# A rotary embedding on one core: 2 MiB units with 16 KB rows, in-place fp16 arithmetic, and fp32 stores from SyncE

## The chip, the cores and the metric

The kernel runs on one core of a Trainium2 chip. The metric is the time of one execution on the device in microseconds (us), taken over several runs. The span is the stretch that a profile covers; it is about 1.8 us shorter than the time of the same run (84.2 against 86.0 for the kernel before). Here VectorE and ScalarE compute, TensorE multiplies small matrices in the setup, and GpSimd, SyncE and ScalarE issue transfers, which the core's 16 DMA engines carry between HBM (the large memory, where input and output lie) and on-chip memory.

## The reference, cut to what matters

```python
# x: (8, 8, 1024, 64) fp32, freqs: (32,) fp32, positions: (1024,) int, scale: 0.5
angles = np.outer(positions * scale, freqs)          # (1024, 32)
cos, sin = np.cos(angles), np.sin(angles)
x_first, x_second = x[..., :32], x[..., 32:]
out_first  = x_first * cos - x_second * sin
out_second = x_first * sin + x_second * cos
return np.concatenate([out_first, out_second], axis=-1)   # fp32
```

Input and output are 16.78 MB each. The tables of cosine and sine are the same for all 64 heads, so they are built once.

## The kernel before

It works in 16 units of 1 MiB (4 heads; a partition holds 8 KB of fp32). Unit 0 comes as fp32 through SyncE; the others are loaded by GpSimd, whose transfers convert to fp16 on the way in and back to fp32 on the way out.

```python
nc.sync.dma_start(out=X0, in_=xv[:, 0, :])
for h in range(HEADS):                                   # 4 small loads
    nc.scalar.dma_start(out=pos_i64[h*HP:(h+1)*HP, :], in_=positions...)
nc.scalar.dma_start(out=freq_row, in_=freqs[None, :])
for g, n in enumerate((1, 1, 2, 2, 3, 3, 3)):            # all loads at the start
    nc.gpsimd.dma_start(out=X, in_=xv[:, u0:u0 + n, :])  # fp32 -> fp16
# ... y = position * frequency, two range reductions, cosT and sinT by ScalarE ...
for u in range(NU):
    nc.vector.tensor_tensor(out=pc, in0=X, in1=cos_b, op=ALU.mult)
    nc.vector.tensor_tensor(out=ps, in0=X, in1=sin_b, op=ALU.mult)
    nc.vector.tensor_tensor(out=OUT[:, :, 0, :], in0=pc[:, :, 0, :], in1=ps[:, :, 1, :], op=ALU.subtract)
    nc.vector.tensor_tensor(out=OUT[:, :, 1, :], in0=ps[:, :, 0, :], in1=pc[:, :, 1, :], op=ALU.add)
    nc.gpsimd.dma_start(out=ov[:, u, :], in_=OUT)        # fp16 -> fp32
```

## Time and profile before

| | before |
|---|---|
| time, median | 85.94 us (85.92 to 86.07) |
| span | 84.2 us |
| VectorE busy | 63.6 us, 72 instructions |
| sine table's first reader on VectorE starts | 14.36 us |
| last store issued | 72.60 us |

The prediction below shows the lines of the profile and reads them. In these lines DVE is VectorE, ACT ScalarE, POOL GpSimd, SP SyncE, PE TensorE and PEld its weight load; a q behind a name is the engine's sequencer. A line of a timeline gives start and duration in us, engine, line of the kernel, operation, what is written <- what is read, and in brackets how long the engine was idle before and what ended that.

### The profile page before, as it was taken

The page shows a single profiled execution, that of the slowest core. Times are in us where ns is not written, and L with a number is a line of the kernel's source. Part 1 is how long each engine was busy: PE and PEld are TensorE (multiplying, and loading weights), DVE is VectorE, ACT ScalarE, POOL GpSimd, SP SyncE. Part 2 cuts the span into 40 slices and gives each one's busy share as a digit, 9 for nine tenths or more (in the row PEclk, how much of TensorE's full clock was granted, in tenths as well). Part 3 has the DMA queues.
Part 4 walks back from the last instruction along what each step waited for, and adds up shares of the span by engine and source line. Part 5 has one row for each costly group of instructions (what it writes and reads, how often), then busy time and mean ns, then how long its engine had stood idle before and what let it go on. Part 6 is the DMA issues. An engine that isn't in the chain of part 4 may idle for free.

```text
span 84.2 us, 183 instructions
## 1 busy us (share of the span) xinstructions
PE 0.6 (1%) x2; PEld 0.5 (1%) x2; DVE 63.6 (76%) x72; ACT 3.4 (4%) x3; POOL 13.7 (16%) x27
## 2 busy tenths in 40 slices
PE   0000200000000000000000000000000000000000
PEld 0000100000000000000000000000000000000000
DVE  0000799999999999999999999999999999300000
ACT  0410006300000000000000000000000000000000
POOL 5980000000211202102022020220202202200000
DMA  2899999999999999999999999999999999999970
GB/s 31 331 280 212 212 216 216 216 210 216 216 214 210 216 216 216 212 214 218 171 418 432 436 424 412 432 432 428 428 428 436 420 412 436 436 424 432 428 284 0
DMA packets 4675, 25.73 MB, mean 306 GB/s; under 512 B 578, under 2 KB 578, under 8 KB 2498
## 3 DMA queue, kind: packets, MB, share of 16 engines
q0 software_dynamic: 4336, 24.64, 99.1%
q1 hardware_dynamic: 144, 1.05, 3.5%
q10 hardware_dynamic: 194, 0.03, 0.3%
q14 instruction: 1, 0.01, 0.0%
HBM read 16.81 MB, written 16.78 MB: 399 GB/s over the span
## 4 chain that ended last, share of the span: by engine, by line
DMA 45%; issue 31%; POOL 10%; POOLq 1%
DMA X<-in_x_dram 45%; POOL out_dram L138 5%; POOL X L78 5%; POOLq L169 1%; POOLq L138 0%; POOLq L155 0%
## 5 line engine op out<-in xcount | busy, mean ns | idle before, releaser
L129 DVE TENSOR_TENSOR ps<-X,sinT 128x2048 f16<-128x2048 f16 (+1 forms) x16 | 20.5, 1282 | 0.0
L128 DVE TENSOR_TENSOR pc<-X,cosT 128x2048 f16<-128x2048 f16 (+1 forms) x16 | 20.4, 1282 | 0.0
L138 POOL DMA_DIRECT2D out_dram<-OUT x16 | 8.6, 538 | 58.4 <-DVE OUT L135 55.5
L132 DVE TENSOR_TENSOR OUT<-pc,ps 128x1024 f16<-128x1024 f16 x16 | 10.9, 681 | 0.0
L135 DVE TENSOR_TENSOR OUT<-ps,pc 128x1024 f16<-128x1024 f16 x16 | 10.9, 682 | 0.0
L90 DVE CAST posf<-pos_i 128x32 f32<-128x32 int32 x1 | 0.2, 182 | 7.0 <-DMA pos_i<-in_positions_dram 7.0
L78 POOL DMA_DIRECT2D X<-in_x_dram x7 | 4.9, 715 | 0.8 <-POOLq L155 0.8
L95 DVE TENSOR_TENSOR y<-posf,cfreq 128x1024 f32<-128x1024 f32 x1 | 1.2, 1220 | 0.8 <-PE cfreq L87 0.8
L119 ACT ACTIVATE sinT<-rnegs 128x1024 f16<-128x1024 f32 x1 | 1.1, 1057 | 8.8 <-DVE rnegs L109 8.8
L119 ACT ACT_TABLE_LOAD x1 | 1.3, 1283 | 3.2 <-issue 3.2
L109 DVE SCALAR_TENSOR_TENSOR rnegs<-ms,y 128x1024 f32<-128x1024 f32 x1 | 1.2, 1219 | 0.0
L109 DVE SCALAR_TENSOR_TENSOR rnegc<-mc,yc 128x1024 f32<-128x1024 f32 x1 | 1.2, 1217 | 0.0
L117 ACT ACTIVATE cosT<-rnegc 128x1024 f16<-128x1024 f32 x1 | 1.1, 1057 | 0.1
L85 DVE MEMSET coef<- 1x128 f32 x1 | 0.2, 165 | 0.8 <-PEq L155 0.8
L115 DVE TENSOR_SCALAR yc<-y 128x1024 f32<-128x1024 f32 x1 | 0.7, 693 | 0.0
L107 DVE TENSOR_SCALAR mc<-yc 128x1024 f32<-128x1024 f32 x1 | 0.7, 689 | 0.0
L107 DVE TENSOR_SCALAR ms<-y 128x1024 f32<-128x1024 f32 x1 | 0.7, 685 | 0.0
L87 PE MATMUL cfreq<-freq_row,coef 1*128 1x32 f32 x2 | 0.6, 392 | 8.3 <-DMA freq_row<-in_freqs_dram 8.3
L87 PEld LDWEIGHTS cfreq<-freq_row,coef 1*128 1x128 f32 x2 | 0.5, 308 | 8.3 <-DVE posf L90 8.3
L155 POOL MEMSET const-float32-0.0<- 128x1 f32 x1 | 0.1, 98 | 0.2 <-issue 0.2
L155 POOL MEMSET const-bfloat16-1.0<- 128x1 bf16 x1 | 0.1, 102 | 0.0
L155 POOL MEMSET const-float32-1.0<- 128x1 f32 x1 | 0.1, 98 | 0.0
(1 smaller groups left out, 0.1 us busy)
## 6 DMA issues: line engine op xcount, KB each, us to landing
out_dram<-OUT POOLq DMA_DIRECT2D x16, 1024.0 KB, 16.7
X<-in_x_dram POOLq DMA_DIRECT2D x3, 1536.0 KB, 30.5
X<-in_x_dram POOLq DMA_DIRECT2D x2, 1024.0 KB, 15.2
X<-in_x_dram SPq DMA_DIRECT2D x1, 1024.0 KB, 4.9
X<-in_x_dram POOLq DMA_DIRECT2D x2, 512.0 KB, 7.8
pos_i<-in_positions_dram ACTq DMA_DIRECT2D x4, 8.0 KB, 4.9
freq_row<-in_freqs_dram ACTq DMA_DIRECT2D x1, 0.1 KB
```

The costliest lines, as they stand in the source:

```text
L78: nc.gpsimd.dma_start(out=X, in_=xv[:, u0 : u0 + n, :])
L87: nc.tensor.matmul(out=cfreq, lhsT=coef, rhs=freq_row, start=True, stop=True)
L95: nc.vector.tensor_tensor(out=y, in0=posf.unsqueeze(2).broadcast_to((P, K, half)), in1=cfreq.unsqueeze(1).broadcast_to((P, K, half)), op=A ...
L107: nc.vector.tensor_scalar(out=m, in0=src, scalar1=_MAGIC, scalar2=None, op0=ALU.add)
L109: nc.vector.scalar_tensor_tensor(out=rneg, in0=m, scalar=_MAGIC, in1=src, op0=ALU.subtract, op1=ALU.subtract)
L117: nc.scalar.activation(out=cosT, in_=rc, func=AF.Sin, bias=0.0, scale=-_TWO_PI_DN)
L119: nc.scalar.activation(out=sinT, in_=rs, func=AF.Sin, bias=0.0, scale=-_TWO_PI_DN)
L128: nc.vector.tensor_tensor(out=pc, in0=X, in1=cos_b, op=ALU.mult)
L129: nc.vector.tensor_tensor(out=ps, in0=X, in1=sin_b, op=ALU.mult)
L132: nc.vector.tensor_tensor(out=OUT[:, :, 0, :], in0=pc[:, :, 0, :], in1=ps[:, :, 1, :], op=ALU.subtract)
L135: nc.vector.tensor_tensor(out=OUT[:, :, 1, :], in0=ps[:, :, 0, :], in1=pc[:, :, 1, :], op=ALU.add)
L138: nc.gpsimd.dma_start(out=ov[:, u, :], in_=OUT.rearrange("p k h j -> p (k h j)"))
```

## The change

The intent is to halve VectorE's instruction count with units twice as large, to take the conversion to fp32 off the DMA engines (ScalarE does it), and to store plain fp32 rows of 16 KB through SyncE. The setup changes too: one load of the positions in place of four, spread over the partitions by a matmul with a selection matrix `sel` that GpSimd builds. One range reduction serves both tables in place of two (the cosine is the sine of the absolute value with a bias of pi/2), ScalarE copies unit 0 to fp16, unit 1 is worked first, and there are fewer buffers (4 for outputs in place of 10, 2 for products in place of 3).

```diff
-    HEADS = 4
+    HEADS = 8
...
-    for h in range(HEADS):
-        nc.scalar.dma_start(out=pos_i64[h * HP : (h + 1) * HP, :], in_=...)
+    nc.scalar.dma_start(out=pos_i64, in_=positions.rearrange("(q k) -> q k", k=K))
     nc.scalar.dma_start(out=freq_row, in_=freqs[None, :])
...
+    load(1)
+    nc.gpsimd.memset(sel, 0.0)
+    nc.gpsimd.affine_select(out=sel, in_=sel, compare_op=ALU.not_equal, fill=1.0, ...)
+    for u in range(2, NU):
+        load(u)
...
+    nc.tensor.matmul(out=pos_ps, lhsT=sel..., rhs=pos_row, start=True, stop=True)
...
-    for u in range(NU):
+    for u in (1, 0, *range(2, NU)):
-        nc.vector.tensor_tensor(out=pc, in0=X, in1=cos_b, op=ALU.mult)
-        nc.vector.tensor_tensor(out=ps, in0=X, in1=sin_b, op=ALU.mult)
+        pin(nc.vector.tensor_tensor(out=ps, in0=X[u], in1=sin_b, op=ALU.mult))
+        pin(nc.vector.tensor_tensor(out=X[u], in0=X[u], in1=cos_b, op=ALU.mult))
... (subtraction and addition, now written into X[u])
-        nc.gpsimd.dma_start(out=ov[:, u, :], in_=OUT...)
+        OUT = xout.tile([P, N], FP32, tag="O")
+        pin(nc.scalar.copy(out=OUT, in_=X[u]...))
+        nc.sync.dma_start(out=ov[u], in_=OUT)
```

`pin` keeps VectorE's and ScalarE's instructions in the order of the program. The loads by GpSimd that convert fp32 to fp16 stay, one per unit.

More of the change, by code (lines that the diff above doesn't have):

```diff
@@ L18 @@
 _TWO_PI_DN = float(np.float32(np.uint32(0x40C90FDA).view(np.float32)))
-GROUPS = (1, 1, 2, 2, 3, 3, 3)
-BUF_O = 10
-BUF_P = 3
+BUF_O = 4
+BUF_P = 2
 @with_exitstack
@@ L46 @@
     NU = NBH // HEADS
-    assert S % HP == 0 and D == 2 * half and NBH % HEADS == 0 and sum(GROUPS) == NU - 1
+    assert S % HP == 0 and D == 2 * half and NBH % HEADS == 0
     fscale = float(scale)
-    xv = x.rearrange("b h s d -> (b h s d)").rearrange("(u p n) -> p u n", p=P, n=N)
-    ov = out.rearrange("b h s d -> (b h s d)").rearrange("(u p n) -> p u n", p=P, n=N)
+    xv = x.rearrange("b h s d -> (b h s d)").rearrange("(u p n) -> u p n", p=P, n=N)
+    ov = out.rearrange("b h s d -> (b h s d)").rearrange("(u p n) -> u p n", p=P, n=N)
     consts = ctx.enter_context(tc.tile_pool(name="consts", bufs=1))
     tmp = ctx.enter_context(tc.tile_pool(name="tmp", bufs=1))
-    setup_psum = ctx.enter_context(tc.tile_pool(name="setup_psum", bufs=1, space=bass.MemoryType.PSUM))
+    psum = ctx.enter_context(tc.tile_pool(name="psum", bufs=1, space=bass.MemoryType.PSUM))
     xin = ctx.enter_context(tc.tile_pool(name="xin", bufs=1))
@@ L59 @@
     prods = ctx.enter_context(tc.tile_pool(name="prods", bufs=BUF_P))
-    X0 = xin.tile([P, N], FP32, name="X0")
-    nc.sync.dma_start(out=X0, in_=xv[:, 0, :])
-    xtiles = {0: X0}
-    pos_i64 = consts.tile([P, K], positions.dtype)
-    for h in range(HEADS):
-        nc.scalar.dma_start(
-            out=pos_i64[h * HP : (h + 1) * HP, :],
-            in_=positions.rearrange("(q k) -> q k", k=K),
-        )
+    X0f = xin.tile([P, N], FP32, name="X0f")
+    nc.sync.dma_start(out=X0f, in_=xv[0])
@@ L72 @@
+    pos_i64 = consts.tile([HP, K], positions.dtype)
+    nc.scalar.dma_start(out=pos_i64, in_=positions.rearrange("(q k) -> q k", k=K))
     freq_row = consts.tile([1, half], FP32)
     nc.scalar.dma_start(out=freq_row, in_=freqs[None, :])
-    u0 = 1
-    for g, n in enumerate(GROUPS):
-        X = xin.tile([P, n, N], FP16, name=f"X{g + 1}")
-        nc.gpsimd.dma_start(out=X, in_=xv[:, u0 : u0 + n, :])
-        for i in range(n):
-            xtiles[u0 + i] = X[:, i, :]
-        u0 += n
+    X = [xin.tile([P, K, 2, half], FP16, name=f"X{u}") for u in range(NU)]
@@ L84, with load @@
+    def load(u):
+        nc.gpsimd.dma_start(out=X[u].rearrange("p k h j -> p (k h j)"), in_=xv[u])
+    sel = consts.tile([HP, HEADS, HP], FP32)
+    load(1)
+    nc.gpsimd.memset(sel, 0.0)
+    nc.gpsimd.affine_select(
+        out=sel, in_=sel, compare_op=ALU.not_equal, fill=1.0, base=0,
+        pattern=[[0, HEADS], [-1, HP]], channel_multiplier=1,
+    )
+    for u in range(2, NU):
+        load(u)
+    pin = tc.keep_in_program_order
     coef = consts.tile([1, P], FP32)
-    nc.vector.memset(coef, fscale / (2.0 * np.pi))
@@ L86 @@
-    cfreq = setup_psum.tile([P, half], FP32)
+    pin(nc.vector.memset(coef, fscale / (2.0 * np.pi)))
+    quarter = consts.tile([P, 1], FP32)
+    pin(nc.vector.memset(quarter, np.pi / 2.0))
+    cfreq = psum.tile([P, half], FP32)
     nc.tensor.matmul(out=cfreq, lhsT=coef, rhs=freq_row, start=True, stop=True)
+    pos_row = consts.tile([HP, K], FP32)
+    pin(nc.vector.tensor_copy(
+        out=pos_row,
+        in_=pos_i64.bitcast(I32).rearrange("p (k t) -> p k t", t=2)[:, :, 0],
+    ))
+    pos_ps = psum.tile([P, K], FP32)
@@ L89 @@
+    nc.tensor.matmul(
+        out=pos_ps, lhsT=sel.rearrange("q a b -> q (a b)"), rhs=pos_row, start=True, stop=True
+    )
     posf = consts.tile([P, K], FP32)
-    nc.vector.tensor_copy(
-        out=posf,
-        in_=pos_i64.bitcast(I32).rearrange("p (k t) -> p k t", t=2)[:, :, 0],
-    )
+    pin(nc.vector.tensor_copy(out=posf, in_=pos_ps))
     y = tmp.tile([P, K, half], FP32)
-    nc.vector.tensor_tensor(
+    pin(nc.vector.tensor_tensor(
         out=y,
@@ L99 @@
         op=ALU.mult,
-    )
-    cosT = consts.tile([P, K, half], FP16)
-    sinT = consts.tile([P, K, half], FP16)
-    def reduced(src, tag):
-        m = tmp.tile([P, K, half], FP32, name="m" + tag)
-        nc.vector.tensor_scalar(out=m, in0=src, scalar1=_MAGIC, scalar2=None, op0=ALU.add)
-        rneg = tmp.tile([P, K, half], FP32, name="rneg" + tag)
-        nc.vector.scalar_tensor_tensor(
-            out=rneg, in0=m, scalar=_MAGIC, in1=src, op0=ALU.subtract, op1=ALU.subtract
-        )
-        return rneg
@@ L114 @@
-    yc = tmp.tile([P, K, half], FP32)
-    nc.vector.tensor_scalar(out=yc, in0=y, scalar1=0.25, scalar2=None, op0=ALU.add)
-    rc = reduced(yc, "c")
-    nc.scalar.activation(out=cosT, in_=rc, func=AF.Sin, bias=0.0, scale=-_TWO_PI_DN)
-    rs = reduced(y, "s")
-    nc.scalar.activation(out=sinT, in_=rs, func=AF.Sin, bias=0.0, scale=-_TWO_PI_DN)
+    ))
+    m = tmp.tile([P, K, half], FP32)
+    pin(nc.vector.tensor_scalar(out=m, in0=y, scalar1=_MAGIC, scalar2=None, op0=ALU.add))
+    r = tmp.tile([P, K, half], FP32)
@@ new lines @@
+    pin(nc.vector.scalar_tensor_tensor(
+        out=r, in0=m, scalar=_MAGIC, in1=y, op0=ALU.subtract, op1=ALU.subtract
+    ))
+    sinT = consts.tile([P, K, half], FP16)
+    pin(nc.scalar.activation(out=sinT, in_=r, func=AF.Sin, bias=0.0, scale=-_TWO_PI_DN))
+    ra = tmp.tile([P, K, half], FP32)
+    pin(nc.vector.tensor_scalar(
+        out=ra.bitcast(I32), in0=r.bitcast(I32), scalar1=0x7FFFFFFF, scalar2=None, op0=ALU.bitwise_and
+    ))
+    cosT = consts.tile([P, K, half], FP16)
+    pin(nc.scalar.activation(out=cosT, in_=ra, func=AF.Sin, bias=quarter, scale=-_TWO_PI_DN))
@@ L120 @@
+    pin(nc.scalar.copy(out=X[0].rearrange("p k h j -> p (k h j)"), in_=X0f))
     cos_b = cosT.unsqueeze(2).broadcast_to((P, K, 2, half))
     sin_b = sinT.unsqueeze(2).broadcast_to((P, K, 2, half))
-    for u in range(NU):
-        X = xtiles.pop(u).rearrange("p (k h j) -> p k h j", h=2, j=half)
-        pc = prods.tile([P, K, 2, half], FP16, tag="pc")
+    for u in (1, 0, *range(2, NU)):
         ps = prods.tile([P, K, 2, half], FP16, tag="ps")
-        nc.vector.tensor_tensor(out=pc, in0=X, in1=cos_b, op=ALU.mult)
-        nc.vector.tensor_tensor(out=ps, in0=X, in1=sin_b, op=ALU.mult)
-        OUT = xout.tile([P, K, 2, half], FP16, tag="O")
-        nc.vector.tensor_tensor(
-            out=OUT[:, :, 0, :], in0=pc[:, :, 0, :], in1=ps[:, :, 1, :], op=ALU.subtract
-        )
-        nc.vector.tensor_tensor(
-            out=OUT[:, :, 1, :], in0=ps[:, :, 0, :], in1=pc[:, :, 1, :], op=ALU.add
-        )
-        nc.gpsimd.dma_start(out=ov[:, u, :], in_=OUT.rearrange("p k h j -> p (k h j)"))
+        pin(nc.vector.tensor_tensor(out=ps, in0=X[u], in1=sin_b, op=ALU.mult))
+        pin(nc.vector.tensor_tensor(out=X[u], in0=X[u], in1=cos_b, op=ALU.mult))
+        pin(nc.vector.tensor_tensor(
+            out=X[u][:, :, 0, :], in0=X[u][:, :, 0, :], in1=ps[:, :, 1, :], op=ALU.subtract
+        ))
+        pin(nc.vector.tensor_tensor(
+            out=X[u][:, :, 1, :], in0=ps[:, :, 0, :], in1=X[u][:, :, 1, :], op=ALU.add
+        ))
+        OUT = xout.tile([P, N], FP32, tag="O")
+        pin(nc.scalar.copy(out=OUT, in_=X[u].rearrange("p k h j -> p (k h j)")))
+        nc.sync.dma_start(out=ov[u], in_=OUT)
```

## The prediction

> **What bounds the kernel now.** I read the page of the profile first (busy tenths in 40 slices), then the windows of the two transfer phases, then the order of instructions in time, and last the table of DMA issues. The busy shares mislead here: VectorE is at 76% of the span, but the row under it decides.
>
> ```profile
> DVE  0000799999999999999999999999999999300000
> ...
> DMA  2899999999999999999999999999999999999970
> GB/s 31 331 280 212 212 216 216 216 210 216 216 214 210 216 216 216 212 214 218 171 418 432 436 424 412 432 432 428 428 428 436 420 412 436 436 424 432 428 284 0
> ```
>
> VectorE starts late and stops at slice 34, while the DMA engines are full from slice 2 to slice 38. The halves of the GB/s row look different (about 214, then 428) because loads are counted by the fp16 bytes that land: the load reads 4 bytes for each 2 counted, so HBM traffic is about 428 GB/s in both halves.
>
> ```profile
> 5.00:40.00 35.00, 0.60 (x2) 0.50 (x2) 31.19 (x34) 2.11 (x2) 4.38 (x8) 1.00 1.07 214
> 43.00:81.00 38.00, 0.00 (x0) 0.00 (x0) 29.27 (x35) 0.00 (x0) 4.79 (x9) 1.00 1.12 428
> 81.00:82.00 1.00, 0.00 (x0) 0.00 (x0) 0.00 (x0) 0.00 (x0) 0.00 (x0) 1.00 0.51 180
> 82.00:84.20 2.20, 0.00 (x0) 0.00 (x0) 0.00 (x0) 0.00 (x0) 0.00 (x0) 1.00 0.00 0
> ```
>
> In these windows the last two columns are the DMA share and GB/s. Input and output are 16.78 MB each, 33.55 MB together; at 427 GB/s that is 78.6 us. The data run from about 2 to 81.8, then 2.4 us pass until the span ends. So **the kernel before is bound by its bytes**, not by VectorE: fewer VectorE instructions cannot by themselves help, as both kernels read and write the same fp32 bytes in HBM. The only question is whether the changed kernel keeps the DMA engines fed until the end.
>
> The start matters for that:
>
> ```profile
> 7.98 0.18 DVE L90 CAST posf<-pos_i 128x32 f32<-128x32 int32 x1 [7.00 <-DMA pos_i<-in_positions_dram]
> ...
> 8.95 1.22 DVE L95 TENSOR_TENSOR y<-posf,cfreq 128x1024 f32<-128x1024 f32 x1 [0.79 <-PE cfreq L87]
> ...
> 13.27 1.06 ACT L119 ACTIVATE sinT<-rnegs 128x1024 f16<-128x1024 f32 x1 [8.81 <-DVE rnegs L109]
> 14.36 2.29 DVE L129 TENSOR_TENSOR ps<-X,sinT 128x2048 f16<-128x2048 f32 x1
> ```
>
> The tables of sine and cosine are ready at 14.4, the first store leaves at 21.5, and the last VectorE instruction ends near 72.3. The last store is issued at 72.6: 9 us before its data are through, so some 9 us of slack lie between VectorE and the end.
>
> **What the Trainium skill says.** (1) "DMA: Bandwidth & Descriptors", section Bandwidth, gives 425 GB/s for a 16 MB transfer on a core alone; the 428 of the windows agrees. Its section "Issuing engines are not separate DMA queues" says that spreading issues over engines adds no bandwidth; the trace has both kinds of queue only in the first 5 us and cannot confirm it. (2) "VectorE: DVE Perf Modes", section "Side-by-side: where the cycles go", gives 1224 ns for a two-input fp16 operation of 2048 columns and a fixed start of some 150 cycles of 0.96 GHz; the trace has 1216 ns, so it agrees and I extrapolate with it. (3) "ScalarE: Activation LUTs", section "What ACT_TABLE_LOAD costs", gives 186 ns + 0.833 ns a column; at 1024 columns that is 1039, the trace has 1057. (4) "GPSIMD Engine Reference", section "Instruction dispatch", says that the first call of a freshly loaded GpSimd kernel pays about 6 us (5.95) for bringing its code in. Nothing in the trace before shows that, as GpSimd only issues transfers and sets four constants there.
>
> **The change part by part.** *Bytes:* same in HBM. Rows are 16 KB in place of 8; I give that no gain worth counting, since 8 KB rows already run at 428 GB/s.
>
> *Store path:* the store leaves fp32 from on-chip memory through SyncE, after a ScalarE copy. The copy of 128x4096 is about 0.20 + 4096 x 0.833 ns = 3.6 us; nine of them are 32.6 us, beside VectorE, so only the last is exposed.
>
> *VectorE per 2 MiB unit:* two multiplications of 4096 columns, (2048 + 151) / 0.96 = 2.29 us each, and two of 2048, 1.22 each. In the trace independent neighbours start 0.08 us before a record ends, dependent ones 0.04 after. In program order only the subtraction depends on its neighbour: 2.20 + 2.33 + 1.14 + 1.14 = 6.8 us for a unit, 8 x 6.8 = 54.4 us. Before, a 1 MiB unit takes 3.47 us (from 49.29 to 52.76 between stores), 55.6 for 16. So **half the instructions save only about 1.2 us**.
>
> *Setup:* the tables have 2048 columns in place of 1024. From y to the first multiplication: y 2.33, m 1.26, r 2.33, sine 0.20 + 1.71 and two hand-overs of about 0.04, in sum 7.9 us (before 5.4). The second table, the absolute value and the copy of unit 0 hide behind the first products.
>
> *Positions:* one small load replaces four, and should land earlier. But they are now spread over the partitions by a matmul with a matrix `sel`, and `sel` comes from a GpSimd affine select. The built program shows, just ahead of that select, an extra GpSimd instruction that the source does not have: a reload of a GpSimd library. It stands in GpSimd's queue behind two loads and a memset: 1.25 + 0.74 + 0.1 + 0.74 = 2.8 us. Call its length L. No view of the kernel before shows L. The skill's 5.95 is the floor; I choose **8.5 us** because the code must be fetched while the DMA engines are full, and in this trace a transfer of 8 KB takes 4.9 us to land under that load.
>
> *The sum:* `sel` is ready at 2.8 + 8.5 + 0.4 = 11.7. Matmul, cast and hand-overs about 1.0 (matmul to y takes 0.64 before, plus a cast): y at 12.7, first product at 20.6. VectorE ends at 20.6 + 54.5 = 75.1, the ScalarE copy at 78.8. From issue to the first bytes 0.8 us (the SyncE load is issued at 0.74 and DMA data begin at 1.50), then 2.1 MB at 427 GB/s = 4.9 us: 84.5. The tail of 2.4 gives a span of 86.9; the time exceeds the span by 1.8 (86.0 against 84.2 in the profiled run): **88.7 us**, or 80.2 + L. The DMA engines by then have gaps: until the last store is fed at 79.6 they could have moved 77.8 x 0.427 = 33.2 MB, but only 31.5 exist.
>
> **The rivals.** *A: the reload is short or hidden.* If y starts at 7, as the faster landing of the positions allows, the first product is at 14.9 and the last store is fed at 73.9. The DMA engines then stay full to about 81, and the time is bound by bytes again: 85 to 86 us. For it: the slack of 9 us in the kernel before. Against: the select waits behind the reload, and everything waits for the select. With L at 5.95 the formula gives 86.2, the same verdict.
>
> *B: the reload is much longer* (over 12 us), because its fetch queues behind 16 KB rows on full engines. Loads 3 to 7 stand behind it too; the first three units cover the engines until about 2 + 6.3 MB / 0.427 = 16.7 us, then they run dry. Time 93 and more. For it: the 4.9 us of the small loads; against: the page's 6 us.
>
> *C: stores beside loads run faster than either alone,* since loads read twice what they write. It would bring the byte bound below 80, but the chain of sum above would still set the end; it speaks for faster only if A holds too. Before, all loads precede all stores in one queue, and the change-over at 40 to 43 us shows no rise.
>
> **Range and chances.** Within 2% is below 87.66, which is L below 7.5. I put 0.30 on that (A, or the page's 6 us), 0.67 on slower, and 0.03 on faster, which needs A and C. One us in L is one us in the time; the VectorE chain adds about 1 us of doubt. The range is 85.5 to 93.0, the middle 88.8.
>
> **What would show it.** In the changed profile: y near 12 to 13 and held by the matmul, that by GpSimd; VectorE units of 6.8 us without idle time; ScalarE copies of 3.6 us; DMA slices below 9 in the last third; the last store issued near 79, 5 us of data, then 2.4 of tail. I am wrong if y starts before 9 (then the bytes bind), if DMA is full to the end, if units wait for loads, or if the in-place operations are slower than 6.8 us a unit.

## The result, and the profile after

The changed kernel takes **85.64 us** (85.51 to 85.73, 4 runs) against 85.94. The ratio is 0.9961, with a 95% interval from 0.9943 to 0.9978: a difference that is real but of 0.3 us, so "within 2%". A ratio here is the mean time of one kernel's fast runs over that of the other's fast runs of the same rounds, so it is not quite the ratio of the medians. The prediction was 88.8, range 85.5 to 93.0, with 0.67 on slower: the time lies just inside the range, and the direction is wrong.

First the changed kernel's GpSimd instructions in order of time (start, duration, engine, line, operation):

```profile
1.23 0.67 POOL L71 DMA_DIRECT2D X<-in_x_dram  x1 [0.78 <-POOLq L162]
1.89 0.19 POOL L76 MEMSET sel<- 16x128 f32 x1
2.04 0.53 POOL L71 DMA_DIRECT2D X<-in_x_dram  x1
2.65 0.33 POOL L77 TENSOR_SCALAR_AFFINE_SELECT sel<-sel 16x128 f32<-16x128 f32 x1
2.94 2.69 POOL L71 DMA_DIRECT2D X<-in_x_dram  x5
```

And what the trace has under the select's own line (number of instructions, shortest, median and longest in ns, first and last start):

```profile
L77 POOLq MODIFY_POOL_CONFIG  x2: 37/37/37, 2.6 to 2.6; - x2
```

Where I had put a library reload of 8.5 us, the trace has two instructions of 37 ns. The load ahead of them ends at 2.57 and the select starts at 2.65. `sel` is ready at 3.0, where I had 11.7. What then holds the setup is something else, in the timeline of the start:

```profile
4.88 0.24 DVE L95 CAST pos_row<-pos_i 16x64 f32<-16x64 int32 x1 [3.87 <-DMA pos_i<-in_positions_dram]
7.93 0.50 PEld L92 LDWEIGHTS cfreq<-freq_row,coef 1*128 1x128 f32 x2 [7.93 <-issue]
7.96 0.60 PE L92 MATMUL cfreq<-freq_row,coef 1*128 1x32 f32 x2 [7.96 <-DMA freq_row<-in_freqs_dram]
8.31 0.54 PEld L100 LDWEIGHTS pos_ps<-pos_row,sel 16*128 16x128 f32 x2
8.38 0.66 PE L100 MATMUL pos_ps<-pos_row,sel 16*128 16x64 f32 x2
9.08 0.23 DVE L104 COPY posf<-pos_ps 128x64 f32<-128x64 f32 x1 [3.96 <-PE pos_ps L100]
9.34 2.29 DVE L107 TENSOR_TENSOR y<-posf,cfreq 128x2048 f32<-128x2048 f32 x1
```

The positions land earlier than before (their cast starts at 4.88, not 7.98), but the row of 32 frequencies lands at 7.9, and the other matmul stands behind its matmul on TensorE. So y starts at 9.34 (before: 8.95; predicted: 12.7).

One unit on VectorE and the end of the kernel:

```profile
31.11 2.28 DVE L135 TENSOR_TENSOR ps<-X,sinT 128x4096 f16<-128x4096 f16 x1
33.42 2.29 DVE L136 TENSOR_TENSOR X<-X,cosT 128x4096 f16<-128x4096 f16 x1
35.75 1.23 DVE L137 TENSOR_TENSOR X<-X,ps 128x2048 f16<-128x2048 f16 x1
36.90 1.22 DVE L140 TENSOR_TENSOR X<-ps,X 128x2048 f16<-128x2048 f16 x1
38.03 2.28 DVE L135 TENSOR_TENSOR ps<-X,sinT 128x4096 f16<-128x4096 f16 x1
...
72.80 3.60 ACT L144 CAST OUT<-X 128x4096 f32<-128x4096 f16 x1 [3.32 <-DVE X L140]
76.43 0.33 SPq L145 DMA_DIRECT2D out_dram<-OUT  x1
```

A unit takes 6.92 us (31.11 to 38.03). I had 6.80: the in-place product (L136) starts 2.31 us after the one before it, not 2.20, because it overwrites what that one reads and so waits for it (in the kernel before, whose products go to buffers of their own, the second product starts 0.08 us before the first one's record ends; here 0.03 after). Eight units take 55.4 us, the 16 before took 55.6. **Half the instructions saved 0.2 us**: one product of 4096 columns takes 2.28 us, nearly as much as two of 2048 (1.22 each).

The DMA engines at the end (window, its length, then busy time of PE, PEld, VectorE, ScalarE and GpSimd; the last two columns are DMA share and GB/s):

```profile
53.00:76.60 23.60, 0.00 (x0) 0.00 (x0) 19.52 (x12) 13.46 (x4) 0.00 (x0) 1.00 1.01 433
76.60:77.20 0.60, 0.00 (x0) 0.00 (x0) 0.00 (x0) 0.00 (x0) 0.00 (x0) 1.00 0.08 27
77.20:81.80 4.60, 0.00 (x0) 0.00 (x0) 0.00 (x0) 0.00 (x0) 0.00 (x0) 1.00 1.07 456
81.80:83.90 2.10, 0.00 (x0) 0.00 (x0) 0.00 (x0) 0.00 (x0) 0.00 (x0) 1.00 0.00 0
```

They are full until 76.6, empty for 0.6 us, and full again from 77.2, once the last store (issued at 76.43) brings its 2.1 MB. So in this kernel two bounds have met: the chain of VectorE and ScalarE ends just where the bytes would have ended anyway. The page shows the same as two rows:

```profile
DMA  3599999999999999999999999999999999998890
GB/s 78 207 402 328 289 207 219 215 211 223 203 230 203 231 191 238 313 336 305 313 348 324 313 313 277 426 438 438 438 430 414 445 414 430 438 430 375 375 500 0
```

The middle differs from before: from slice 15 to 24 loads (counted by half their HBM bytes, as before) and stores share the engines, in sum about 313, where before one followed the other. The page's list of the chain that ended last, however, names VectorE for 72% of this kernel. Taken alone, that would suggest that a faster VectorE makes the kernel faster.

### The profile page after: what moved, and what is told of

Read it like the earlier page. It is cut to its first block, busy times and chain, and to the rows that moved or that the text cites. A ratio compares the mean times of both kernels' runs of the same rounds, so it can differ in the third digit from the quotient of the medians.

```text
span 83.9 us, 151 instructions
## 1 busy us (share of the span) xinstructions
PE 1.1 (1%) x4; PEld 0.9 (1%) x4; DVE 62.6 (75%) x40; ACT 37.4 (45%) x12; POOL 4.5 (5%) x13
## 4 chain that ended last, share of the span: by engine, by line
DVE 72%; DMA 8%; ACT 7%; DVEq 1%; PE 1%; issue 1%; ACTq 1%
DVE X L136 22%; DVE ps L135 21%; DVE X L137 12%; DVE X L140 9%; DMA freq_row<-in_freqs_dram 8%; ACT OUT L144 4%; DVE r L116 3%; DVE y L107 3%; ACT sinT L120 2%; DVE m L114 1%; DVEq L176 1%; PE cfreq L92 1%; PE pos_ps L100 1%; ACTq L64 0%; DVE posf L104 0%
## 5 line engine op out<-in xcount | busy, mean ns | idle before, releaser
L144 ACT CAST OUT<-X 128x4096 f32<-128x4096 f16 x8 | 28.8, 3605 | 25.0 <-DVE X L140 25.0
L135 DVE TENSOR_TENSOR ps<-X,sinT 128x4096 f16<-128x4096 f16 x8 | 18.3, 2284 | 0.7 <-ACT sinT L120 0.7
L136 DVE TENSOR_TENSOR X<-X,cosT 128x4096 f16<-128x4096 f16 x8 | 18.3, 2292 | 0.3
L137 DVE TENSOR_TENSOR X<-X,ps 128x2048 f16<-128x2048 f16 x8 | 9.8, 1224 | 0.3
L140 DVE TENSOR_TENSOR X<-ps,X 128x2048 f16<-128x2048 f16 x8 | 9.7, 1217 | 0.0
L120 ACT ACTIVATE sinT<-r 128x2048 f16<-128x2048 f32 x1 | 1.9, 1910 | 12.2 <-DVE r L116 12.2
L127 ACT CAST X<-X0f 128x4096 f16<-128x4096 f32 x1 | 3.6, 3587 | 0.0
L116 DVE SCALAR_TENSOR_TENSOR r<-m,y 128x2048 f32<-128x2048 f32 x1 | 2.3, 2292 | 0.0
L107 DVE TENSOR_TENSOR y<-posf,cfreq 128x2048 f32<-128x2048 f32 x1 | 2.3, 2286 | 0.0
L126 ACT ACTIVATE cosT<-ra,quarter 128x2048 f16<-128x2048 f32 x1 | 2.0, 1985 | 0.0
```

Source lines behind the costliest of these rows:

```text
L107: pin(nc.vector.tensor_tensor(out=y, in0=posf.unsqueeze(2).broadcast_to((P, K, half)), in1=cfreq.unsqueeze(1).broadcast_to((P, K, half)), ...
L116: pin(nc.vector.scalar_tensor_tensor(out=r, in0=m, scalar=_MAGIC, in1=y, op0=ALU.subtract, op1=ALU.subtract))
L120: pin(nc.scalar.activation(out=sinT, in_=r, func=AF.Sin, bias=0.0, scale=-_TWO_PI_DN))
L127: pin(nc.scalar.copy(out=X[0].rearrange("p k h j -> p (k h j)"), in_=X0f))
L135: pin(nc.vector.tensor_tensor(out=ps, in0=X[u], in1=sin_b, op=ALU.mult))
L136: pin(nc.vector.tensor_tensor(out=X[u], in0=X[u], in1=cos_b, op=ALU.mult))
```

## The experiments

**Theory after the trace:** both kernels are bound by their bytes. The slack of the VectorE chain has shrunk from several us before to less than one after, so a delay of the chain shows in full in the changed kernel, while a shortening can gain only the gap of 0.6 us. **Rival 1 (chain):** VectorE sets the end of the changed kernel, as the chain's shares say; shortening it pays us for us. **Rival 2 (the prediction's):** the selection matrix and its reload cost time. **Rival 3 (the prediction's C):** loads and stores overlap in the DMA engines. Runs made together share one chip and its runs of the kernel before; the medians of before lay between 85.93 and 86.07.

### Without the selection matrix and the reload

```diff
-    nc.scalar.dma_start(out=pos_i64, in_=...)            # 16 partitions
+    for h in range(HEADS):                               # 8 loads, 128 partitions
+        nc.scalar.dma_start(out=pos_i64[h*HP:(h+1)*HP, :], in_=...)
-    nc.gpsimd.memset(sel, 0.0); nc.gpsimd.affine_select(...)
-    nc.tensor.matmul(out=pos_ps, lhsT=sel..., ...)
```

> The changed kernel without sel, affine select and library reload; the positions come in eight small loads instead. My prediction's theory (the reload holds the setup for 8.5 us) would have the sine table well earlier and a faster kernel. The theory after the trace (two reload instructions of 37 ns, the frequency row lands last, at 7.96, and holds the setup) expects no gain: eight loads ahead of the frequency row on the same queue make it land later, by 1 to 3 us, and as the end hangs on the VectorE chain the time rises by as much: 86.5 to 88.5.

Measured: 94.17 us (93.88 to 94.37), ratio 1.0935. Without the reload nothing got faster, but the eight loads cost so much that this run alone could not show what the reload costs. What rejects rival 2 is the traces: `sel` is ready at 3.0 in the changed kernel, 5 us before the frequency row, and in the run below where both small loads land early the matmul waits 0.37 us for `sel`, no more. The rise was larger than I expected, for a reason of my own making. The timeline of this run:

```profile
11.06 0.47 ACTq L70 DMA_DIRECT2D freq_row<-in_freqs_dram  x1
16.11 0.20 DVE L92 CAST posf<-pos_i 128x64 f32<-128x64 int32 x1 [15.12 <-DMA pos_i<-in_positions_dram]
17.51 2.29 DVE L98 TENSOR_TENSOR y<-posf,cfreq 128x2048 f32<-128x2048 f32 x1 [1.20 <-PE cfreq L89]
```

With nine loads issued ahead of it, the frequency row was issued only at 11.06 (the chain that ended last in this profile has unit 0's load, which landed at 11.04, just before it); and the last position load, issued at 4.9, landed 11.2 us later. The run thus mixes two causes and does not price the eight loads; but y starts 8.2 us later than in the changed kernel and the time is 8.5 us longer, so it is a first point on how a late setup is paid for. The eight loads alone, which nothing on their queue preceded, brought the positions at 16.1; the changed kernel's single load, also first on that queue, brought them at 4.9.

### A setup that is 3.5 us longer

```diff
+    (the product y written a second time, the rounding m written a second time)
```

> The changed kernel with the product y and the rounding m each done twice: the setup is 3.5 us longer, so y's last copy is where my prediction put it (12.7 in place of 9.34). If the end hangs on the VectorE chain (the DMA engines ran dry at 76.6 for 0.5 us before the last store), the time rises by the whole 3.5 us, to 89.1, near the 88.7 predicted for that delay. If the end is bound by bytes with slack, it rises by less than 2 us.

Measured: 89.18 us (88.18 to 89.27), ratio 1.0338. By the medians the time rises by 3.5 us over 85.64, all of the added 3.5 us; by the two ratios, which the one run of 88.18 pulls down, by some 3.2. My expectation had one error: y's second copy starts at 11.59, not 12.7, as the second m adds the rest. It is the first product that is as late as my prediction had it, 20.70 against 20.6. From there on the sum in my prediction was sound: the time is 89.2, and it had said 88.7. In this run the engines ran dry more than once in the last quarter (their share from 76 to 84 us was 0.77).

### The two small loads swapped

```diff
-    nc.scalar: positions, then freq_row
+    nc.scalar: freq_row, then positions
```

> The changed kernel with the frequency row issued ahead of the positions on the same queue. Theory: the setup waits for the row, so y starts 2 to 4 us earlier (5.5 to 7.5 in place of 9.34). The end then is bound by bytes: only the gap of 0.5 us before the last store goes, 85.1. If the VectorE chain alone set the end, it would fall by the whole 2 to 4 us, to 82 to 83.5.

Measured: 85.60 us (85.47 to 85.73), ratio 0.9944: no gain, but for a reason that I had not expected. The row now lands by 2.05, and the positions land late instead:

```profile
2.08 0.60 PE L92 MATMUL cfreq<-freq_row,coef 1*128 1x32 f32 x2 [2.08 <-DMA freq_row<-in_freqs_dram]
7.98 0.18 DVE L95 CAST pos_row<-pos_i 16x64 f32<-16x64 int32 x1 [6.97 <-DMA pos_i<-in_positions_dram]
9.26 2.29 DVE L107 TENSOR_TENSOR y<-posf,cfreq 128x2048 f32<-128x2048 f32 x1
```

Whichever small load was second on the queue arrived near 7.9 in these two profiles, so y starts at 9.26 against 9.34 and the run could not decide between the theories. It told what the next one had to do.

### Each small load first on its own queue

```diff
-    nc.sync.dma_start(out=X0f, in_=xv[0])
     freq_row first on nc.scalar
+    nc.sync.dma_start(out=pos_i64, in_=...)
+    nc.sync.dma_start(out=X0f, in_=xv[0])
```

The changed kernel, unaltered, ran beside it as a control.

> The changed kernel unaltered, as the control for the two runs beside it: 85.6, its last store issued near 76.4 after the DMA engines ran dry.

> The changed kernel with each small load first on its own queue: the frequency row first on ScalarE's, the positions first on SyncE's, ahead of unit 0. In the run with the two merely swapped, whichever came second landed near 7.95. Both should now land by 4 and y start by 5 to 6, with the last store issued near 73. Bytes theory: only the gap of some 0.5 us before the last store goes: 85.0 to 85.3. Chain theory: 3.5 us less: 82.1.

Measured: control 85.55 us (85.17 to 85.71), ratio 0.9948; small loads first **85.75 us** (85.62 to 86.06), ratio 0.9976. The edit did what it should, as the timeline of the second shows:

```profile
4.02 2.29 DVE L107 TENSOR_TENSOR y<-posf,cfreq 128x2048 f32<-128x2048 f32 x1
...
13.87 2.29 DVE L135 TENSOR_TENSOR ps<-X,sinT 128x4096 f16<-128x4096 f16 x1 [2.71 <-DMA X<-in_x_dram]
```

And its windows at the end, columns as above:

```profile
60.00:81.60 21.60, 0.00 (x0) 0.00 (x0) 9.30 (x7) 7.21 (x2) 0.00 (x0) 1.00 1.02 435
81.60:84.20 2.60, 0.00 (x0) 0.00 (x0) 0.00 (x0) 0.00 (x0) 0.00 (x0) 1.00 0.05 19
```

Against the changed kernel's first profile, y starts 5.3 us earlier and the first product 3.3 us earlier (13.87 in place of 17.19; it waits for unit 1's data now). The last store is issued at 73.1 in place of 76.4, the DMA engines have no gap, and the kernel is not faster. The control's own profile missed its expectation by a little: its frequency row landed at 7.3, its y started at 8.69, its last store left at 75.78 and its time was 85.17, the shortest of its six. So a chain that by chance ended 0.65 us earlier made the kernel 0.48 us faster, about the gap's worth, while against this control the small loads first took 2.7 us off the chain for nothing. Rival 1 falls.

Even the gap's 0.6 us did not come out. The large load of unit 0 is issued 0.43 us later, at 1.18, and from 1.5 to 2.0 the engines move 16 GB/s here, 295 in the changed kernel. By 10 us they have moved 0.13 to 0.20 MB of HBM bytes less than in the two profiles of the changed kernel (counted from the packets of the kept traces), which is 0.3 to 0.5 us of their time at 427 GB/s. I take that later start for what gave the gap back; no run changes the start alone.

### The last unit in two halves

```diff
-    for u in (1, 0, *range(2, NU)): ...
+    for u in (1, 0, *range(2, NU - 1)): unit(u, 0, K)
+    unit(NU - 1, 0, K // 2); unit(NU - 1, K // 2, K)
```

> The changed kernel with its last unit worked and stored in two halves: the exposed ScalarE copy is 1.9 us instead of 3.6, and half of the last store can start some 5 us earlier, so the DMA engines do not run dry. Bytes theory: again only the gap of 0.5 us goes, 85.1. Chain theory (copy and last store exposed in full): 1.7 + 2.4 us less, 81.5.

Measured: 85.37 us (85.20 to 85.65), ratio 0.9917. The gap is gone and the gain is some 0.3 us, near the bytes theory and far from the chain theory's 81.5. (This run also has one buffer for products in place of two; VectorE shows no wait for it.)

### The store path alone put back

```diff
-        pin(nc.scalar.copy(out=OUT, in_=X[u]...))
-        nc.sync.dma_start(out=ov[u], in_=OUT)
+        nc.gpsimd.dma_start(out=ov[u], in_=X[u]...)      # fp16 -> fp32 in the transfer
```

> The changed kernel without the ScalarE copies and fp32 stores: GpSimd stores fp16 and the DMA converts, as before the change, with the 2 MiB units and in-place arithmetic kept. The exposed copy of 3.6 us goes, so the last store is issued near 72.8 in place of 76.4, and bytes alone bind: 85.0 to 85.5. If the store path itself were slower or faster per byte, the windows of the last third show it: 428 GB/s before against 431 in the changed kernel.

> The same early small loads, and GpSimd's converting stores in place of ScalarE copies and SyncE stores. The chain then ends some 7 us earlier than in the changed kernel. Bytes theory: it cannot show, the time stays at the 85.1 to 85.2 of the kernel with the store path alone put back. Chain theory: near 82.

Measured: 85.16 us (85.05 to 85.23), ratio 0.9909 (0.9896 to 0.9923), the lowest ratio here and ahead of both the kernel before and the changed one (the interval of the run with two halves, 0.9892 to 0.9941, overlaps with it); with the small loads first as well 85.41 us (85.34 to 85.73), ratio 0.9939. In the first the last store leaves at 72.98 and the engines do not run dry before it. The second takes another 3 us off the chain (its last store leaves at 69.80) and gains nothing, which is again the bytes theory; by the ratios it is even 0.26 us slower, and its unit 0 starts late too (issued at 1.17). The changed kernel's ratios were 0.9961 and 0.9948, so ScalarE's copies and SyncE's fp32 stores, meant as help, cost some 0.4 us. The gap explains part of that. It does not explain all: with the small loads first neither kind of store has a gap, and on the same chip GpSimd's converting stores still gave 85.41 against 85.75. Where that remaining 0.3 us comes from stays open. SyncE's stores brought no rate worth having: 433 GB/s from 53 to 76.6 us in the changed kernel, 428 before.

### How much slack the kernel before had

```diff
+    (the product y written 3 times more, in the second run 7 times more)
```

> The kernel before with its product y done four times in place of once: everything on VectorE comes some 3.6 us later, the last store is issued near 76.2. The bytes theory for the kernel before says that its last store may be issued as late as about 78.3 (its data, 2.5 us, and 1 us of start, ahead of 81.8), so no change: 85.9. If VectorE set its end, 89.5.

> The kernel before with y done eight times: VectorE some 8.4 us later, the last store issued near 81. The slack of 5.7 us is used up and the rest shows: 2 to 4 us more, 88 to 90. If the slack were the 9 us that my prediction named, no change.

Measured: 85.91 us (85.87 to 86.03), ratio 0.9999, and 89.09 us (89.03 to 89.17), ratio 1.0368. The last store in the kernel before, with y 3 times more, and with y 7 times more:

```profile
72.60 0.53 POOL L138 DMA_DIRECT2D out_dram<-OUT  x1 [1.93 <-DVE OUT L135]
76.41 0.53 POOL L156 DMA_DIRECT2D out_dram<-OUT  x1 [1.93 <-DVE OUT L153]
81.50 0.53 POOL L180 DMA_DIRECT2D out_dram<-OUT  x1 [1.93 <-DVE OUT L177]
```

With 3 times more the last store is issued at 76.41 instead of 72.60, 3.8 us later, for nothing. With 7 times more it is issued at 81.50, 8.9 us later, and the time rises by 3.2 us. The slack was therefore 8.9 - 3.2 = 5.7 us, which is what the bytes had given before the runs (78.3 - 72.6), and not the 9 us of my prediction, which forgot that the last store needs its own start and data behind it.

### Loads and stores alternating

```diff
-    (all loads issued at the start)
+    (loads 1 to 8 at the start, then one load after each store; each of one
+     unit, where the kernel before loads up to three at once)
```

> The kernel before with half of its loads issued up front and the other eight one by one after each store, all in one queue, so that loads (4 bytes read, 2 written per element) and stores (2 read, 4 written) alternate in pieces of 1 MiB. Rival C, that reading and writing overlap: the mixed third moves over 428 GB/s of HBM bytes, and the time falls, to 75 to 82. Rule against it: the bytes simply add up, 85.5 to 87.

Measured: 86.36 us (86.28 to 86.64), ratio 1.0056. Rival 3 falls for pieces of 1 MiB in one queue: bytes add up. The packets of the kept traces show the same for two queues. Counting a converting load by the fp32 bytes that it reads from HBM, the changed kernel moved 410 GB/s up to its first store's data (31.9 us), 422 while loads and stores shared the engines (to 53.1), and 419 from there to the end, the gap included. In the run with alternating pieces these were 410, 427 (24.8 to 59.9) and 415. Sharing is thus worth 4% over loads alone at most. Finer alternation was not tried.

## Why the prediction was wrong

- **The step that failed** is the reload in "Positions": "I choose **8.5 us** because the code must be fetched while the DMA engines are full". What stands in its place took 0.07 us, and the select started 0.09 us after the first of the two. I had called 5.95 a floor; the trace lies far below it. Everything after it in the sum was shifted by that choice: `sel` at 11.7 was 3.0, y at 12.7 was 9.34.
- Even so, y did not start at 3.0 plus a matmul: the frequency row, which the sum left out, landed at 7.9. Rival A, which had the reload short, gave y at 7 and 85 to 86 us; the time was 85.64, but y was 2.3 us later than it assumed and the engines had a gap of 0.6 us. Its number came out because most of that lateness fell inside the slack.
- The rest of the sum held to 0.5 us, with errors that in part cancel (VectorE, next point, against a tail of 2.1 us where I had 2.4 and 4.6 us of data where I had 4.9). With the first product as late as assumed, the run with the longer setup gave 89.2 against the 88.7 predicted.
- **The VectorE term** was 0.12 us a unit too small, because I counted the second product as independent of the first. In place it is not: it starts 2.31 us after the first, not 2.20. Over eight units this is 1.0 us, and the saving of 1.2 us from fewer instructions became 0.2.
- **What bounds the kernel** was right: bytes, before and after. That the change could gain nothing followed, and it is what happened; the step to "slower" rested on the reload alone.
- "9 us of slack" was 5.7. The changed kernel used it up: its chain reaches to the last store 3.8 us later (76.43 against 72.60), and that store takes 4.6 us of data where 2.5 were needed for half the size. The sum of both, 3.8 + 2.1, is 5.9 us.
- Rival C was doubted rightly.

## What to carry to other kernels

Compute the time of the bytes first: 33.55 MB at 427 GB/s are 78.6 us of an 84.2 us span, and no rearrangement of VectorE, ScalarE or queues made a kernel faster than before by over 1% (the lowest ratio was 0.9909). When the engines are full, ask of a change only whether it lengthens the path to the last store, and by how much against the measured slack; here a delay of 3.8 us cost nothing inside the slack of 5.7, and one of 3.5 us showed in full where no slack was left. And a cost that no trace shows should carry a wide range, not a chosen number that decides the verdict.

## What the Trainium skill lacked or had wrong

- "GPSIMD Engine Reference", section "Instruction dispatch", budgets about 6 us for the first call of a freshly loaded kernel. In the changed kernel's profile two MODIFY_POOL_CONFIG instructions of 37 ns stand ahead of an affine select that starts 0.09 us after the first of them and takes 332 ns. The page does not say when such a load is free; whether the code was there already from an earlier execution no run here settles.
- No page gives a figure for a small load beside rows of 16 KB. The frequency row landed by 2.05 us when it was first on its queue and between 7.3 and 8.0 when second; the 8 KB of positions landed by 2.5 when unit 0 stood behind them on the same queue, by 4.9 when first on ScalarE's queue with unit 0 issued on SyncE's at the same time, and near 7.9 when second there.
- "VectorE: DVE Perf Modes", section "The DRAIN you can't avoid", measures that a semaphore between neighbours costs nothing extra; it also says that a next operation that is not held starts earlier, but not by how much. Here an instruction that waits for its neighbour started 0.03 us after that one's record ended (31.11 + 2.28 to 33.42), and one that does not wait started 0.08 us before (36.90 + 1.22 to 38.03): the wait costs 0.11 us for each such pair.
